# One block of 128 rows per partition instead of two blocks of 65 and 63 rows, and the logits in one transfer

## The chip, the cores and the metric

The kernel runs on one NeuronCore of one Trainium2 chip. The metric is the time of one execution on the device, in microseconds (us); lower is better. Three runs of the kernel before took 239.15 to 239.20 us, median 239.16 us. The profile comes from one more execution, which took 239.38 us, of which the span that the profile covers is 237.6 us.

## What is computed

The reference is the gate of a mixture of experts. For each of 16 x 1024 tokens it takes the softmax over 8 logits, keeps the two largest probabilities, scales them to a sum of one, and writes the token's 512 values twice, once times each of the two weights, the smaller first:

```
probs = np.exp(router_logits - logits_max)
probs = probs / np.sum(probs, axis=-1, keepdims=True)
topk_indices = np.argsort(probs, axis=-1)[..., -k:]
topk_probs = np.take_along_axis(probs, topk_indices, axis=-1)
topk_probs = topk_probs / np.sum(topk_probs, axis=-1, keepdims=True)
x_expanded = x[:, :, np.newaxis, :].repeat(k, axis=2)
return (x_expanded * topk_probs[..., np.newaxis]).astype(np.float32)
```

With k = 2, x is 16 x 1024 x 512 float32 (33.55 MB, 2048 B a token), the logits are 16 x 1024 x 8 float32 (0.52 MB, 32 B a token), and the output is 16 x 1024 x 2 x 512 float32 (67.11 MB, 4096 B a token).

## The kernel before

The 16384 tokens are "rows" here. They are spread over the 128 partitions of the on-chip memory, 128 rows to each (M = 128), in two groups: GROUPS = [65, 63] (line 16). Group 0 is the first 128 x 65 rows of x, and partition p has rows 65 p to 65 p + 64 of it; group 1 is the remaining 128 x 63 rows, and partition p has rows 63 p to 63 p + 62 of those. Lines 87 to 94 build these views of x, output and logits: x_v, o_v and rl_v, one entry a group. So what one partition reads in one transfer is one contiguous run of memory, and the runs of neighbouring partitions lie a fixed distance apart, which this document calls the pitch. The pitch is the group's rows times the bytes of a row:

| | group 0 | group 1 |
|---|---|---|
| x | 65 x 2048 B = 130 KiB | 63 x 2048 B = 126 KiB |
| output | 65 x 4096 B = 260 KiB | 63 x 4096 B = 252 KiB |
| logits | 65 x 32 B = 2080 B | 63 x 32 B = 2016 B |

Tiles on the chip: xs holds up to 65 rows of x per partition, osp has space for 18 rows of output (OSP), and WA holds the two weights of every row. The logits are loaded into the last row of osp, and the scratch space of the selection is the two rows ahead of it.

What runs, in the order in which it is issued:

- Loads: all by SyncE (SP), line 112, in pieces of LOADS = [[6, 28, 31], [32, 31]] rows per partition. After the piece of 6 rows, SP issues the two transfers of logits (lines 105 and 106), then the pieces of 28 and 31 rows.
- Weights: top2_weights works on the logits of both groups at once on VectorE (DVE), with max and min over halves (lines 53 to 66), and takes the two sigmoids of the difference on ScalarE (ACT), lines 67 and 68. Its first instruction, line 53, waits for both transfers of logits.
- Products and stores: STORES (lines 23 to 37) lists by hand, for each group, pieces of 2, 16, 16, 16 and 15 rows (group 1: 16, 16, 16, 15), the place where a piece's products go (osp, or rows of xs that have been used up), how many of its rows ACT multiplies (line 135) while DVE multiplies the rest (line 127), and the queue that issues the store (line 138): ACT's for the first piece, SP's for all others.
- The loads of group 1 overwrite xs. The one of 32 rows waits for the store of the second 16-row piece of group 0, which has its products in xs, and the one of 31 rows waits for the store of the last 15 rows.

A transfer is spread over the core's 16 DMA engines by partition, and each partition's run is one packet of up to 64 KiB (32 rows of x, or 16 rows of output); one more small packet per engine reports the end of the transfer. That makes 128 + 16 = 144 packets a transfer, and 16 x 144 = 2304 in all, the number on the page.

Of the kernel before, what the change touches and what calls it, by code (L numbers as in the profile page):

```python
# [1 line left out]

# [4 lines left out]

F32 = mybir.dt.float32
ALU = mybir.AluOpType
ACTF = mybir.ActivationFunctionType  # L10
P = 128
E = 8
D = 512


GROUPS = [65, 63]
M = sum(GROUPS)


LOADS = [[6, 28, 31], [32, 31]]  # L20


STORES = [
    [
        (2, ("osp", 0), 0, "ACT"),
        (16, ("osp", 2), 0, "SP"),
        (16, ("x", 2), 0, "SP"),
        (16, ("osp", 0), 4, "SP"),
        (15, ("x", 35), 0, "SP"),
    ],  # L30
    [
        (16, ("osp", 0), 1, "SP"),
        (16, ("x", 0), 0, "SP"),
        (16, ("osp", 0), 4, "SP"),
        (15, ("x", 33), 0, "SP"),
    ],
]
OSP = 18


def top2_weights(nc, scratch, logits, WA):

    used = [0]

    def cut(n):
        a = scratch[:, used[0] : used[0] + M * n].rearrange("p (m n) -> p m n", n=n)
        used[0] += M * n
        return a

    a, b = logits[:, :, 0:4], logits[:, :, 4:8]  # L50
    hi = cut(4)
    lo = b
    nc.vector.tensor_tensor(hi, a, b, op=ALU.max)  # L53
    nc.vector.tensor_tensor(lo, a, b, op=ALU.min)  # L54
    n = 4
    while n > 1:
        n //= 2
        a, b = hi[:, :, 0:n], hi[:, :, n : 2 * n]
        nhi, nlo, tmp = cut(n), cut(n), cut(n)
        nc.vector.tensor_tensor(tmp, lo[:, :, 0:n], lo[:, :, n : 2 * n], op=ALU.max)  # L60
        nc.vector.tensor_tensor(nlo, a, b, op=ALU.min)  # L61
        nc.vector.tensor_tensor(nlo, nlo, tmp, op=ALU.max)  # L62
        nc.vector.tensor_tensor(nhi, a, b, op=ALU.max)  # L63
        hi, lo = nhi, nlo
    dlt = cut(1)
    nc.vector.tensor_tensor(dlt, hi, lo, op=ALU.subtract)  # L66
    nc.scalar.activation(WA[:, :, 0], dlt[:, :, 0], ACTF.Sigmoid, scale=-1.0)  # L67
    nc.scalar.activation(WA[:, :, 1], dlt[:, :, 0], ACTF.Sigmoid, scale=1.0)  # L68


@with_exitstack
def kernel(
    ctx: ExitStack,
    tc: tile.TileContext,
    x: bass.AP,
    router_logits: bass.AP,
    k: bass.AP,
    out: bass.AP,
):
    nc = tc.nc  # L80
    N = x.shape[0] * x.shape[1]
    assert int(k) == 2 and router_logits.shape[-1] == E and x.shape[2] == D
    assert N == P * M
    xf = x.rearrange("b s d -> (b s) d")
    of = out.rearrange("b s k d -> (b s) k d")
    rf = router_logits.rearrange("b s e -> (b s) e")
    x_v, o_v, rl_v = [], [], []
    t0 = 0
    for n in GROUPS:
        t1 = t0 + P * n  # L90
        x_v.append(xf[t0:t1].rearrange("(p m) d -> p m d", p=P))
        o_v.append(of[t0:t1].rearrange("(p m) k d -> p m k d", p=P))
        rl_v.append(rf[t0:t1].rearrange("(p m) e -> p m e", p=P))
        t0 = t1

    pool = ctx.enter_context(tc.tile_pool(name="pool", bufs=1))
    xs = pool.tile([P, max(GROUPS), D], F32)
    osp = pool.tile([P, OSP, 2, D], F32)
    WA = pool.tile([P, M, 2], F32)

    logits = osp[:, OSP - 1].rearrange("p k d -> p (k d)").rearrange("p (m e) -> p m e", e=E)
    scratch = osp[:, OSP - 3 : OSP - 1].rearrange("p r k d -> p (r k d)")

    def load_logits():
        nc.sync.dma_start(logits[:, : GROUPS[0]], rl_v[0])  # L105
        nc.sync.dma_start(logits[:, GROUPS[0] :], rl_v[1])  # L106

    m0 = 0
    for g, G in enumerate(GROUPS):
        r = 0  # L110
        for n in LOADS[g]:
            nc.sync.dma_start(xs[:, r : r + n, :], x_v[g][:, r : r + n, :])  # L112
            if g == 0 and r < 6 <= r + n:
                load_logits()
                top2_weights(nc, scratch, logits, WA)
            r += n
        assert r == G
        r = 0
        for n, (home, a), by_act, queue in STORES[g]:
            if home == "x":  # L120
                og = xs[:, a : a + 2 * n, :].rearrange("p (r k) d -> p r k d", k=2)
            else:
                og = osp[:, a : a + n]
            v = n - by_act
            w = WA[:, m0 + r : m0 + r + n, :]
            if v:
                nc.vector.tensor_tensor(  # L127
                    og[:, :v],
                    xs[:, r : r + v, :].unsqueeze(2).to_broadcast([P, v, 2, D]),
                    w[:, :v].unsqueeze(3).to_broadcast([P, v, 2, D]),  # L130
                    op=ALU.mult,
                )
            for i in range(v, n):
                for c in range(2):
                    nc.scalar.activation(  # L135
                        og[:, i, c], xs[:, r + i, :], ACTF.Copy, scale=w[:, i, c : c + 1]
                    )
            {"SP": nc.sync, "ACT": nc.scalar}[queue].dma_start(o_v[g][:, r : r + n], og)  # L138
            r += n
        assert r == G  # L140
        m0 += G


# [1 line left out]
_INS = ['x', 'router_logits', 'k']  # L145
_OUTS = [((16, 1024, 2, 512), 'float32')]

_NUMBERS = {'k': 2}


# [26 lines left out]
```

## Time and profile before

| | |
|---|---|
| median of 3 runs | 239.16 us (239.15 to 239.20) |
| the profiled execution | 239.38 us, span 237.6 us |
| bytes read and written | 34.08 MB and 67.11 MB |
| transfers | 5 loads of x, 2 of logits, 9 stores |
| DVE busy | 132.2 us (56% of the span) |
| ACT busy | 13.2 us (6%) |

How to read what is shown below. The page of the profile begins with the busy time of each engine; its second part cuts the span into 40 equal slices, with the mean busy share of the 16 DMA engines in tenths and the GB/s that they moved. The chain of waits goes back from the last instruction and names at each step what released it. The timeline lists instructions by start and duration, SPq being the queue of SyncE, whose time is that of issuing and not of moving data. The view by stretches gives, for chosen stretches of the span, the busy time of the engines, the granted TensorE clock (not used by this kernel), the share that the DMA engines were busy, and GB/s. A packet takes up to some us and seems to be credited whole to the stretch where it falls, so that short stretches swing above and below what was really moved (a share above 1.00 can be met); long ones are better.

### The profile page before, as it was taken

Reading aid. Unit: us, or ns where it says so; the run is one execution under the profiler, and the core shown is the slowest. Engines: PE = TensorE matmul, PEld = TensorE weight load, DVE = VectorE, ACT = ScalarE, POOL = GpSimd, SP = SyncE. Lnnn points to the kernel's source line nnn. Section 1 sums busy time; section 2 is a strip of 40 time slices with the busy share of each in tenths; the row PEclk is TensorE's granted clock in tenths of the full one; section 3 lists DMA queues with packets and bytes.
Section 4 is the critical chain, followed back from the end, with each engine's and each line's share of the span. In section 5 each row is a group of like instructions: output and inputs, shape, how many; then the busy total and the mean of one; then the engine's idle time right before and its main releaser. Section 6 shows DMA issues by size and latency. Waiting matters only on the chain.

```text
span 237.6 us, 124 instructions
## 1 busy us (share of the span) xinstructions
DVE 132.2 (56%) x20; ACT 13.2 (6%) x21; POOL 0.2 (0%) x4
## 2 busy tenths in 40 slices
DVE  0640599999289999000000009999956999920000
ACT  2000000000080000000000001000006100000000
POOL 0000000000000000000000000000000000000000
DMA  7979989898989989899998989898989989897995
GB/s 265 541 338 488 408 386 535 348 530 353 496 386 441 441 353 530 353 508 414 414 519 353 508 370 502 353 519 353 496 386 419 463 353 530 353 530 342 496 445 217
DMA packets 2304, 101.19 MB, mean 426 GB/s; under 512 B 256, under 2 KB 384, under 8 KB 512
## 3 DMA queue, kind: packets, MB, share of 16 engines
q1 hardware_dynamic: 2160, 100.14, 97.7%
q10 hardware_dynamic: 144, 1.05, 1.0%
HBM read 34.08 MB, written 67.11 MB: 426 GB/s over the span
## 4 chain that ended last, share of the span: by engine, by line
DMA 48%; DVE 39%; SPq 1%; issue 0%; DVEq 0%
DMA xs<-in_x_dram 30%; DVE osp L127 25%; DMA out_dram<-osp 19%; DVE xs L127 14%; SPq L105 0%; SPq L106 0%; SPq L112 0%; SPq L138 0%; DVEq L127 0%
## 5 line engine op out<-in xcount | busy, mean ns | idle before, releaser
L127 DVE TENSOR_TENSOR osp<-xs,WA 128x12288 f32<-128x12288 f32 (+3 forms) x5 | 61.6, 12318 | 68.7 <-DMA xs<-in_x_dram 58.4
L127 DVE TENSOR_TENSOR xs<-xs,WA 128x16384 f32<-128x16384 f32 (+1 forms) x4 | 66.8, 16692 | 0.3
L135 ACT ACTIVATE osp<-xs,WA 128x512 f32<-128x512 f32 x18 | 11.4, 709 | 161.3 <-DMA out_dram<-osp 90.0
L53 DVE TENSOR_TENSOR osp<-osp 128x512 f32<-128x512 f32 x1 | 0.7, 692 | 8.2 <-DMA osp<-in_router_logits_dram 8.2
L67 ACT ACT_TABLE_LOAD x1 | 1.3, 1283 | 0.7 <-PEq L158 0.7
L67 ACT ACTIVATE WA<-osp 128x128 f32<-128x128 f32 x1 | 0.3, 316 | 10.1 <-DVE osp L66 10.1
L54 DVE TENSOR_TENSOR osp<-osp 128x512 f32<-128x512 f32 x1 | 0.7, 693 | 0.0
L60 DVE TENSOR_TENSOR osp<-osp 128x256 f32<-128x256 f32 (+1 forms) x2 | 0.7, 352 | 0.0
L62 DVE TENSOR_TENSOR osp<-osp 128x256 f32<-128x256 f32 (+1 forms) x2 | 0.7, 352 | 0.0
L63 DVE TENSOR_TENSOR osp<-osp 128x256 f32<-128x256 f32 (+1 forms) x2 | 0.7, 352 | 0.0
L61 DVE TENSOR_TENSOR osp<-osp 128x256 f32<-128x256 f32 (+1 forms) x2 | 0.7, 351 | 0.0
L66 DVE TENSOR_TENSOR osp<-osp 128x128 f32<-128x128 f32 x1 | 0.3, 292 | 0.0
L68 ACT ACTIVATE WA<-osp 128x128 f32<-128x128 f32 x1 | 0.3, 298 | 0.0
L158 POOL MEMSET const-bfloat16-1.0<- 128x1 bf16 x1 | 0.1, 102 | 0.0
L158 POOL MEMSET const-uint8-127<- 128x1 uint8 x1 | 0.1, 102 | 0.0
L158 POOL MEMSET const-float32-0.0<- 128x1 f32 x1 | 0.1, 99 | 0.2 <-issue 0.2
L158 POOL MEMSET const-float32-1.0<- 128x1 f32 x1 | 0.1, 99 | 0.0
## 6 DMA issues: line engine op xcount, KB each, us to landing
xs<-in_x_dram SPq DMA_DIRECT2D x2, 7936.0 KB, 40.8
out_dram<-xs SPq DMA_DIRECT2D x2, 7680.0 KB, 27.5
xs<-in_x_dram SPq DMA_DIRECT2D x1, 7168.0 KB, 24.2
xs<-in_x_dram SPq DMA_DIRECT2D x1, 1536.0 KB, 6.0
out_dram<-osp ACTq DMA_DIRECT2D x1, 1024.0 KB, 24.5
osp<-in_router_logits_dram SPq DMA_DIRECT2D x1, 260.0 KB, 6.2
osp<-in_router_logits_dram SPq DMA_DIRECT2D x1, 252.0 KB, 6.4
out_dram<-osp SPq DMA_DIRECT2D x4, 23.9
```

The costliest lines, as they stand in the source:

```text
L53: nc.vector.tensor_tensor(hi, a, b, op=ALU.max)
L54: nc.vector.tensor_tensor(lo, a, b, op=ALU.min)
L60: nc.vector.tensor_tensor(tmp, lo[:, :, 0:n], lo[:, :, n : 2 * n], op=ALU.max)
L61: nc.vector.tensor_tensor(nlo, a, b, op=ALU.min)
L62: nc.vector.tensor_tensor(nlo, nlo, tmp, op=ALU.max)
L63: nc.vector.tensor_tensor(nhi, a, b, op=ALU.max)
L66: nc.vector.tensor_tensor(dlt, hi, lo, op=ALU.subtract)
L67: nc.scalar.activation(WA[:, :, 0], dlt[:, :, 0], ACTF.Sigmoid, scale=-1.0)
L68: nc.scalar.activation(WA[:, :, 1], dlt[:, :, 0], ACTF.Sigmoid, scale=1.0)
L127: nc.vector.tensor_tensor(og[:, :v], xs[:, r : r + v, :].unsqueeze(2).to_broadcast([P, v, 2, D]), w[:, :v].unsqueeze(3).to_broadcast([P, v ...
L135: nc.scalar.activation(og[:, i, c], xs[:, r + i, :], ACTF.Copy, scale=w[:, i, c : c + 1])
L158: nc = _bacc.Bacc("TRN2", target_bir_lowering=False, num_devices=1)
```

## The change

x and output are seen as one block of 128 rows for each partition (xp and op): partition p has rows 128 p to 128 p + 127, of which the first 65 are its share of group 0 and the other 63 of group 1. The entries of x_v and o_v are slices of those views. The pitch becomes 128 x 2048 B = 256 KiB for x and 128 x 4096 B = 512 KiB for the output, for both groups. The logits come in one transfer, 128 x 32 B = 4096 B per partition, and rl_v is gone. The pieces of loads and stores, the tiles, the queues and the arithmetic are as before. A blank line more near the top and three lines less further down shift the numbers of some lines: lines 53 to 68 of before are 54 to 69 after, the one transfer of logits is line 106, and from line 108 on the numbers are the same.

```
-    x_v, o_v, rl_v = [], [], []
+    xp = xf.rearrange("(p m) d -> p m d", p=P)
+    op = of.rearrange("(p m) k d -> p m k d", p=P)
+    x_v, o_v = [], []
     t0 = 0
     for n in GROUPS:
-        t1 = t0 + P * n
-        x_v.append(xf[t0:t1].rearrange("(p m) d -> p m d", p=P))
-        o_v.append(of[t0:t1].rearrange("(p m) k d -> p m k d", p=P))
-        rl_v.append(rf[t0:t1].rearrange("(p m) e -> p m e", p=P))
-        t0 = t1
+        x_v.append(xp[:, t0 : t0 + n])
+        o_v.append(op[:, t0 : t0 + n])
+        t0 += n
...
     def load_logits():
-        nc.sync.dma_start(logits[:, : GROUPS[0]], rl_v[0])
-        nc.sync.dma_start(logits[:, GROUPS[0] :], rl_v[1])
+        nc.sync.dma_start(logits, rf.rearrange("(p m) e -> p m e", p=P))
```

## The prediction

> **What bounds the kernel now.** I read the page's second part first, then the view by stretches, the chain of waits, and the timeline of the start.
>
> ```profile
> span 237.6 us, 124 instructions
> DVE 132.2 (56%) x20; ACT 13.2 (6%) x21; POOL 0.2 (0%) x4
> DMA  7979989898989989899998989898989989897995
> DMA packets 2304, 101.19 MB, mean 426 GB/s; under 512 B 256, under 2 KB 384, under 8 KB 512
> q1 hardware_dynamic: 2160, 100.14, 97.7%
> q10 hardware_dynamic: 144, 1.05, 1.0%
> HBM read 34.08 MB, written 67.11 MB: 426 GB/s over the span
> ...
> 0.00:2.00 2.00, 0.00 (x0) 1.27 (x1) 0.20 (x4) 1.00 0.35 68
> 4.00:6.00 2.00, 0.00 (x0) 0.00 (x0) 0.00 (x0) 1.00 0.97 415
> 2.00:43.00 41.00, 22.76 (x13) 0.52 (x3) 0.00 (x0) 1.00 1.00 426
> 44.00:95.00 51.00, 45.78 (x3) 5.01 (x8) 0.00 (x0) 1.00 1.00 432
> 100.00:140.00 40.00, 0.00 (x0) 0.00 (x0) 0.00 (x0) 1.00 1.00 433
> 235.00:236.00 1.00, 0.00 (x0) 0.00 (x0) 0.00 (x0) 1.00 0.00 0
> ```
>
> No slice of the DMA line is empty, and the two queues together took 98.7% of what sixteen engines could give. In the long stretches, mostly loads in the first, stores in the second, both mixed in the third, the share is 1.00; the rate is 426 GB/s with the start in it and then 432 and 433. At 432 GB/s the 101.19 MB take 101.19 / 432 = 234.2 us. The span has 237.6; the other 3.4 us are the start (the row 0 to 2 us has a share of 0.35, the first load being issued only at 0.73) and the end (nothing is carried after 235). So the time is bytes over rate plus 3.4 us, and no gap is left to close between the first packet and the last. DVE works 132.2 us and is 44% idle; the chain shows what that idleness waits for:
>
> ```profile
> 2.10 24.16 DMA xs<-in_x_dram
> ...
> 26.35 17.24 DVE osp L127
> ...
> 43.61 22.22 DMA out_dram<-osp
> ...
> 95.58 46.42 DMA xs<-in_x_dram
> ...
> 158.32 21.80 DMA out_dram<-osp
> ...
> 193.26 16.16 DVE xs L127
> ```
>
> Each long step of DVE follows a landing of a load or of a store. A slower transfer therefore moves everything behind it by the same amount, and a faster one would do so too; the chain's pieces are only the places where DVE notices.
>
> **The logits.** One transfer in place of two.
>
> ```profile
> 0.73 0.38 SPq L112 DMA_DIRECT2D xs<-in_x_dram  x1
> 1.16 0.43 SPq L105 DMA_DIRECT2D osp<-in_router_logits_dram  x1
> 1.64 0.42 SPq L106 DMA_DIRECT2D osp<-in_router_logits_dram  x1
> 2.10 1.11 SPq L112 DMA_DIRECT2D xs<-in_x_dram  x2
> 8.16 0.69 DVE L53 TENSOR_TENSOR osp<-osp 128x512 f32<-128x512 f32 x1 [8.16 <-DMA osp<-in_router_logits_dram]
> 12.63 2.29 DVE L127 TENSOR_TENSOR osp<-xs,WA 128x2048 f32<-128x2048 f32 x1 [0.58 <-ACT WA L68]
> 14.95 0.37 ACTq L138 DMA_DIRECT2D out_dram<-osp  x1
> ...
> xs<-in_x_dram SPq DMA_DIRECT2D x1, 1536.0 KB, 6.0
> osp<-in_router_logits_dram SPq DMA_DIRECT2D x1, 252.0 KB, 6.4
> ```
>
> SP issues one instruction less: 2.10 - 1.64 = 0.46 us, by which the loads of 28 and 31 rows are issued earlier. That is worth nothing by itself: the load of 6 rows lands at 0.73 + 6.0 = 6.7 us and the engines are busy with it until about then, more than 4 us after the next loads are in the queue. Without that cover it would be the whole 0.46 us. On the engines the bytes stay the same (512 KB). The second transfer of logits lands at 1.64 + 6.4 = 8.0, which leaves 8.0 - 6.7 = 1.3 us for 0.524 MB, against 0.524 / 432 = 1.2 us at the long stretches' rate. What packets of 2 KB and the second report of completion cost is thus at most 0.1 us, and one transfer with 128 + 16 packets less (2304 becomes 2160) cannot save more. I take the 0.1 us, since the engines are the bound and pass it on to the end; its own bounds are 0 and 0.1. On DVE's side line 53 now waits for one transfer; it may start 0.1 us earlier, and so may the first store at 14.95, which shares the engines with loads that are queued in any case.
>
> **The order and the waits.** In the order of instructions every engine has what it had, but for that one issue: DVE 20 operations with the same shapes, ACT its 18 products, nine stores and five loads with the same pieces. The waits on SP's queue stand where they stood: the load of 32 rows waits for the second 16-row store of group 0, the load of 31 rows for the 15-row store, and behind these two wait the stores of group 1. The semaphores that transfers report to go round, and with one transfer less all later ones move by one place; each wait still names the same transfer. No wait is added, so 0 with no bounds to keep.
>
> **The pitch.** This is the part that can matter. What the 16 engines do at the same time is to walk through the runs of 16 different partitions. Before, the starts of neighbouring runs lie 130 or 126 KiB (x) and 260 or 252 KiB (output) apart; only runs 64 or 128 partitions apart have the low 18 bits of their addresses in common. After, all lie 256 KiB and 512 KiB apart: every run starts with the same low 18 (x) or 19 (output) bits. If the memory picks its parallel parts by those bits, engines that are in step ask the same part together. The trace of before has no transfer with such a pitch, so I bound the price. Below: 0, as in the rows of 432 and 433 GB/s, where the engines are the limit; a gain is excluded, since a share of 1.00 leaves none. Above: the only time when all engines are surely in step is the first load, which they begin together. Its first microseconds hold the wait for the first data as well:
>
> ```profile
> 2.00:4.00 2.00, 0.00 (x0) 0.01 (x1) 0.00 (x0) 1.00 0.80 307
> ...
> 5.00:6.00 1.00, 0.00 (x0) 0.00 (x0) 0.00 (x0) 1.00 0.91 387
> ```
>
> At 307 GB/s throughout, the bytes would take 101.19 / 307 = 329.6 us, 95 us more; that is the outermost end and I give it little weight, as most of that row's loss is the wait for first data. In the next two microseconds (row 4 to 6) the packets flow and the engines are still nearly in step, at 415 GB/s. At that rate the output alone takes 67.11 / 415 - 67.11 / 432 = 6.4 us more and x and logits 34.08 / 415 - 34.08 / 432 = 3.2 us more, together 9.6 us. Between 0 and 9.6, nearest to these rows and far from 95, I take the middle, 4.8 us, which is three quarters of what the output, whose pitch is the longer one, would lose alone. It falls on the end in full, because the engines have no pause in which to hide it: later stores first lengthen DVE's two waits for osp (5.11 and 4.64 us) and SP's wait of 26.2 us ahead of the loads of group 1.
>
> ```profile
> 65.95 12.96 DVE L127 TENSOR_TENSOR osp<-xs,WA 128x12288 f32<-128x12288 f32 x1 [5.11 <-DMA out_dram<-osp]
> 180.22 12.96 DVE L127 TENSOR_TENSOR osp<-xs,WA 128x12288 f32<-128x12288 f32 x1 [4.64 <-DMA out_dram<-osp]
> SPq L112 <- DMA out_dram<-xs: 26.2, 1, 26.2
> ```
>
> The Trainium skill has a rule that speaks against this change: DMA: Bandwidth & Descriptors, section Latency and other measured facts, entry on HBM row pitch at large powers of two. Copies between memory tensors gave 207 GB/s in each direction at a pitch of 512 KiB per partition, 164 at 2 MiB, 103 at 4 MiB, and 214 again at 4 MiB padded by 4 KiB; the page calls its mechanism an inference. That before runs at 432 GB/s with pitches 4 KiB off 256 KiB agrees with the padded case; no run here yet shows the other. Taken for the output alone, the rule would give an estimate of 155.3 x (214 / 207 - 1) = 5.3 us more, so a sum of 244.6 us, while the unchanged row of 432 GB/s gives 239.3.
>
> **The sum.** Against the profiled execution of 239.38 us: 239.38 - 0.1 + 0 + 4.8 = 244.1. The median of the runs is 0.22 us under the profiled execution, so the forecast is 243.9 us.
>
> **The rivals.**
>
> The addresses don't matter: the DMA engines set the pace whatever the pitch. For it speaks that the share stays at 1.00 in loads, stores and their mixture, through four different pitches. Against it, that none of the four is a power of two. It gives 239.16 - 0.1 = 239.1 us, no change that can be told. It decides wherever the memory serves each engine's packets faster than the engine asks.
>
> The engines stay in step for good and loads suffer as well. The steps that then grow are the waits for loads in the chain (24.16 and 46.42 us) before the stores. At the worst later microsecond of the first load, 387 GB/s in the row 5 to 6, the bytes take 101.19 / 387 = 261.5 us, 27.3 more: 266.4 us. For it: the rates of 432 and 433 GB/s are so steady that engines, once in step, seem to have little to pull them out of it. Against it: a single microsecond with whole packets credited to it is a poor witness.
>
> The front is shorter: faster. The logits' one issue brings the loads to the engines 0.46 us earlier and the engines start the load of 28 rows that much sooner, with the 0.1 us of packets on top: 239.16 - 0.56 = 238.6 us. It needs the engines to have run dry between 4 and 8 us; the row 4 to 6 with a share of 0.97 speaks against it, and so does the load's landing at 6.7 us.
>
> That the change doesn't do what it says can be left out: the pitches are fixed by the views.
>
> **How the numbers follow.** A moderate loss by the pitch: 0.56, between 239.7 and 250 us. Engines in step for good: 0.12, 250 and above. No effect: 0.26, at 239.1. The shorter front: 0.06, at 238.6. I give the pitch more than half because it changes for every byte at a moment when the transfers have no slack, and the one stretch in which engines are in step is slow. Measured runs differ by 0.05 us, and 0.2% (0.5 us) is about what can be told from no change; faster 0.06, within 0.26, slower 0.68. The range goes from 238.9, just under the case of no effect, to 253, which takes in the 9.6 us at 415 GB/s (248.7) and the beginning of the strong case; the rest of that, about 0.1, and the shorter front are left out. The likeliest case's own range is 239.7 to 250.
>
> **What would show it.** If the forecast holds, the DMA line of the page stays full, the mean falls from 426 to about 417 GB/s with the same MB, and the long stretches show a share of 1.00 at less than 432 GB/s; DVE's busy time stays at 132.2 us. The chain's waits for a store (22.22 and 21.80 us) grow by some 0.6 us for 16 rows, an eighth of 4.8. If the pitch does nothing, the stretches still show 432. The step on the logits is right if line 106 is issued once, the next load at about 1.6 us, and the first weights begin at about 8.1 us. The forecast is wrong if loads slow down and stores don't, or if gaps (shares well under 1.00 in a long stretch) appear.

## The result and the profile after

The changed kernel takes 240.35 us (median of 6 runs, 240.16 to 240.75); the kernel before took 239.18 us in the runs beside it (6 runs, 239.15 to 239.28). The ratio is 1.005, 95% interval 1.0037 to 1.0063. It is slower, as forecast, and inside the range, but by 1.17 us where 4.8 were forecast. The profiled execution took 240.16 us, the lowest of its six; so the profile shows 0.78 us of the loss.

From the page of the kernel after, the span, the DMA line and the totals; then its view by stretches (stretch, its length, busy time of DVE, ACT and POOL, clock, DMA share, GB/s):

```profile
span 238.4 us, 122 instructions
DMA  7979989898989898989798999998999989897994
DMA packets 2160, 101.19 MB, mean 424 GB/s; under 512 B 240, under 2 KB 240, under 8 KB 368
...
44.00:95.00 51.00, 45.79 (x3) 5.01 (x8) 0.00 (x0) 1.00 1.00 432
100.00:140.00 40.00, 0.00 (x0) 0.00 (x0) 0.00 (x0) 1.00 1.02 433
116.00:128.00 12.00, 0.00 (x0) 0.00 (x0) 0.00 (x0) 1.00 1.06 426
```

The bytes are the same, the packets are 144 fewer, and the stretch from 44 to 95 us, where little but stores at the new pitch of 512 KiB is moved, runs at a share of 1.00 and 432 GB/s, to the digit what it was. So a stream of stores does not suffer from the pitch at all. The stretch from 100 to 140 moves the same 433 GB/s, but the engines were busy for 1.02 in place of 1.00. The time between 116 and 128 us holds the difference. The same stretch of the kernel before:

```profile
116.00:128.00 12.00, 0.00 (x0) 0.00 (x0) 0.00 (x0) 1.00 0.99 426
```

Equal bytes (426 GB/s), but the packets took 0.07 x 12 = 0.84 us of every engine's time more. What happens there is read from the chain of waits of the kernel after (start, length, what):

```profile
1.63 24.49 DMA xs<-in_x_dram
...
43.47 22.21 DMA out_dram<-osp
...
95.44 47.27 DMA xs<-in_x_dram
...
158.95 21.88 DMA out_dram<-osp
...
193.97 16.16 DVE xs L127
```

and from its timeline, with the two loads of group 1 in one row whose length runs from the issue of the first to the issue of the second:

```profile
1.16 0.42 SPq L106 DMA_DIRECT2D osp<-in_router_logits_dram  x1
1.63 0.95 SPq L112 DMA_DIRECT2D xs<-in_x_dram  x2
8.12 0.69 DVE L54 TENSOR_TENSOR osp<-osp 128x512 f32<-128x512 f32 x1 [8.12 <-DMA osp<-in_router_logits_dram]
95.44 28.63 SPq L112 DMA_DIRECT2D xs<-in_x_dram  x2
```

In the kernel before the last of these rows was:

```profile
95.58 27.65 SPq L112 DMA_DIRECT2D xs<-in_x_dram  x2
```

At 95.4 us the kernel after is 0.14 us ahead. By the end of the chain's next piece, at 95.44 + 47.27 = 142.7 against 142.0, it is 0.7 us behind, and it stays so: the last step of DVE begins at 193.97 against 193.26. The waits for stores are 22.21 and 21.88 us, against 22.22 and 21.80. The whole loss lies in one piece: the landing of the last 15 rows of group 0, for which the second load waits, comes 28.63 - 27.65 = 1.0 us later. That is the only place in the kernel where the engines change from a long run of stores to loads.

The trace also keeps the size, start and length of every packet, and these narrow it down. In the kernel after, each of the 16 engines carries the 15-row store as eight packets. The last one takes 2.63 to 2.97 us, where the seven ahead of it take 2.27; the first two packets of the load behind it take 2.42 to 2.95 us, where later ones take 2.42. Together that is 0.9 us an engine. In the kernel before, the same packets take at most 2.38 and 2.53 us. The packets of the long stream of stores take 2.42 us in both kernels, although the 16 engines begin theirs within 0.5 us of each other all through it.

### The profile page after: what moved, and what is told of

Read it like the earlier page. It is cut to its first block, busy times and chain, and to the rows that moved or that the text cites. A ratio compares the mean times of both kernels' runs of the same rounds, so it can differ in the third digit from the quotient of the medians.

```text
span 238.4 us, 122 instructions
## 1 busy us (share of the span) xinstructions
DVE 132.2 (55%) x20; ACT 13.2 (6%) x21; POOL 0.2 (0%) x4
## 4 chain that ended last, share of the span: by engine, by line
DMA 49%; DVE 38%; SPq 0%; issue 0%; DVEq 0%
DMA xs<-in_x_dram 30%; DVE osp L127 25%; DMA out_dram<-osp 18%; DVE xs L127 14%; SPq L106 0%; SPq L112 0%; SPq L138 0%; DVEq L127 0%
```

## The experiments

The times of each group were taken on one chip with runs of the kernel before among them. The row that is shown for each is that of the two loads of group 1, as above, because its length tells the loss without the noise of the rest.

**Which part of the change.** Four kernels, each with one part of the change alone or undone.

The pitch of x alone (x_v from one block, the rest as before):

```
-        x_v.append(xf[t0:t1].rearrange("(p m) d -> p m d", p=P))
+        m0 = t0 // P
+        x_v.append(xf.rearrange("(p m) d -> p m d", p=P)[:, m0 : m0 + n])
```

> x is read from one block of 128 rows per partition (pitch 256 KiB), output and logits as before, so that the rows of x that are multiplied are other ones than those that the weights belong to. Theory A (the loss needs both pitches, because it arises where the stores of the last 15 rows of group 0 meet the loads of group 1 and both have the same low address bits): about 239.2 us, and SP's wait ahead of the load of 31 rows stays at 26.2 us. Theory B (the pitch of the output alone): 239.2 us. Theory C (the pitch of x alone): about 240.4 us, the wait at 27 us. Theory D (the one transfer of logits, which moves the engines' phases): 239.2 us.

The pitch of the output alone:

```
-        o_v.append(of[t0:t1].rearrange("(p m) k d -> p m k d", p=P))
+        m0 = t0 // P
+        o_v.append(of.rearrange("(p m) k d -> p m k d", p=P)[:, m0 : m0 + n])
```

> The output is written as one block of 128 rows per partition (pitch 512 KiB), x and logits as before, so that rows land in other places than the reference's. Theory A (both pitches needed): about 239.2 us, SP's wait ahead of the load of 31 rows at 26.2 us. Theory B (output alone): about 240.4 us, the wait at 27 us. Theory C (x alone): 239.2 us. Theory D (logits): 239.2 us.

The one transfer of logits alone:

```
-        nc.sync.dma_start(logits[:, : GROUPS[0]], rl_v[0])
-        nc.sync.dma_start(logits[:, GROUPS[0] :], rl_v[1])
+        nc.sync.dma_start(logits, rf.rearrange("(p m) e -> p m e", p=P))
```

> The logits come in one transfer of 4096 B per partition, x and output as before, so that most rows get the weights of others. Theories A, B and C: 0.1 us faster than before, about 239.1 us, with the first weights at 8.1 us. Theory D (the one transfer moves the engines' phases and that costs at the change from stores to loads): about 240.4 us.

The changed kernel with two transfers of logits:

```
-        nc.sync.dma_start(logits, rf.rearrange("(p m) e -> p m e", p=P))
+        rl = rf.rearrange("(p m) e -> p m e", p=P)
+        nc.sync.dma_start(logits[:, : GROUPS[0]], rl[:, : GROUPS[0]])
+        nc.sync.dma_start(logits[:, GROUPS[0] :], rl[:, GROUPS[0] :])
```

> The changed kernel with the logits in two transfers again, from the one block (2080 and 2016 B per partition at a pitch of 4096 B). Theories A, B and C: as slow as the changed kernel or 0.1 us slower, 240.4 to 240.5 us, the load of 31 rows waiting about 27 us. Theory D (logits): about 239.2 us.

| | us (median, range) | ratio to before, 239.23 us |
|---|---|---|
| x alone | 239.68 (239.57 to 239.88) | 1.0018 (1.0009 to 1.0026) |
| output alone | 240.78 (240.30 to 241.00) | 1.0059 (1.0047 to 1.0072) |
| logits alone | 239.31 (239.22 to 239.49) | 1.0003 (0.9994 to 1.0011) |
| x and output, two transfers of logits | 240.71 (240.39 to 240.82) | 1.0056 (1.0043 to 1.0070) |

The row of the two loads of group 1, from the timelines in this order:

```profile
95.85 27.56 SPq L113 DMA_DIRECT2D xs<-in_x_dram  x2
```

```profile
95.36 28.71 SPq L113 DMA_DIRECT2D xs<-in_x_dram  x2
```

```profile
95.36 27.60 SPq L111 DMA_DIRECT2D xs<-in_x_dram  x2
```

```profile
96.05 28.52 SPq L114 DMA_DIRECT2D xs<-in_x_dram  x2
```

The two kernels with the output at 512 KiB have 28.5 to 28.7 us there, the two without it 27.6, as before. Theory A falls: x need not have its new pitch. Theories C and D fall as well; B, the output alone, stands, and x and logits add nothing to it that can be told. One thing none of the theories said: x alone costs 0.45 us. Its profile has the first load land 0.3 us later than before, which is not in the changed kernel. From the views of DMA issues (KB, us to landing) of x alone and of the kernel after:

```profile
xs<-in_x_dram SPq DMA_DIRECT2D x1, 1536.0 KB, 6.3
```

```profile
xs<-in_x_dram SPq DMA_DIRECT2D x1, 1536.0 KB, 6.1
```

**Low bits or distance.** The pitch of 512 KiB is a power of two, and it is also twice the old one. Two kernels with everything else as before, in both of which the last store is cut into 13 and 2 rows, have 128 and 126 rows from one partition's output to the next; in both, rows land elsewhere than the reference's. The two excerpts leave out the lines that cut the last store.

```
+    op = of.rearrange("(p m) k d -> p m k d", p=P)
+    o_v = [op[:, :65], op[:, 65:126]]
+    o_tail = op[:, 126:]
...
```

> x and logits as before, output at a pitch of 512 KiB (128 rows), the last store cut into 13 and 2 rows so that it can be compared with its sister of 504 KiB. Both theories: the loss of the output's pitch is there, about 1.5 us over the time that its sister would have without it, so about 241 us; the chain's piece of waiting for the loads of group 1 at about 48 us.

```
+    op = of[: P * 126].rearrange("(p m) k d -> p m k d", p=P)
+    o_v = [op[:, :65], op[:, 65:]]
+    o_tail = of[P * 126 :].rearrange("(p m) k d -> p m k d", p=P)
...
```

> The same with the output at a pitch of 504 KiB (126 rows; the two rows of each partition that are left over go to the end of the output, so rows land elsewhere than the reference's). Theory low bits (what costs is that all runs start with the same low 19 address bits): 1.2 to 1.5 us faster than the kernel with 512 KiB, the piece of waiting for the loads of group 1 at about 46.5 us. Theory distance (what costs is that neighbouring partitions lie twice as far apart): the same time as with 512 KiB, the piece at about 48 us.

512 KiB: 240.51 us (240.31 to 240.60), ratio 1.0049 (1.0037 to 1.0062) to before, 239.30 us. 504 KiB: 239.22 us (239.12 to 239.61), ratio 1.0000 (0.9991 to 1.0009). The same row from the timelines of 512 and of 504 KiB:

```profile
95.30 28.71 SPq L116 DMA_DIRECT2D xs<-in_x_dram  x2
```

```profile
95.54 27.53 SPq L116 DMA_DIRECT2D xs<-in_x_dram  x2
```

8 KiB less of nearly the same distance takes the whole loss away. It is the low bits.

A third kernel asked whether half the pitch is enough, with two groups of 64 rows:

```
-GROUPS = [65, 63]
+GROUPS = [64, 64]
-LOADS = [[6, 28, 31], [32, 31]]
+LOADS = [[6, 28, 30], [32, 32]]
...
-        (15, ("x", 35), 0, "SP"),
+        (14, ("x", 35), 0, "SP"),
...
-        (15, ("x", 33), 0, "SP"),
+        (16, ("x", 32), 0, "SP"),
```

> Before with two groups of 64 rows each: pitches of 128 KiB for x and 256 KiB for the output, both powers of two but half of the changed kernel's; loads of 6, 28, 30 and 32, 32 rows, stores of 2, 16, 16, 16, 14 and four of 16 rows. All right results. If 18 equal low bits in the output's addresses are enough for the loss: about 240.5 us, the piece of waiting for the loads of group 1 over 47 us. If it takes the 19 bits of 512 KiB: about 239.2 us, the piece at 46.5 us. Between them: a smaller pitch costs less.

239.61 us (239.38 to 240.35), ratio 1.0018 (1.0009 to 1.0027) to 239.21 us, between the two: some 0.4 us. Since the sizes of two stores and two loads differ as well, and x has a pitch of 128 KiB, this is no clean number; it suggests that 256 KiB costs less than 512, and doesn't show it.

**Once per change from stores to loads?** If the loss belongs to that change, a kernel with one change more should lose about twice. The load of 32 rows is cut into 16 and 16, and the first is issued ahead of the last store of group 0; this for the old pitches and for the output at 512 KiB.

```
-LOADS = [[6, 28, 31], [32, 31]]
+LOADS = [[6, 28, 31], [16, 16, 31]]
...
+            if g == 0 and n == 15:
+                n1 = LOADS[1][0]
+                nc.sync.dma_start(xs[:, :n1, :], x_v[1][:, :n1, :])
             {"SP": nc.sync, "ACT": nc.scalar}[queue].dma_start(o_v[g][:, r : r + n], og)
```

> Before, with the load of 32 rows of group 1 cut into 16 and 16, and the first 16 issued ahead of the store of the last 15 rows of group 0, so that the engines change from stores to loads twice in place of once. Both theories: 239.2 us, up to 0.2 us more for one transfer more; it is the reference for its sister with the other output pitch.

> The same with the output at a pitch of 512 KiB. Theory change (each change of the engines from stores to loads costs about 1.5 us at this pitch, and nothing else costs): about 3 us over its sister with the old pitches, 242.2 us. Theory place (something about this one store or this one moment costs, or the loss is spread): about 1.5 us over its sister, 240.7 us.

Old pitches: 240.21 us (239.98 to 240.63), ratio to before (239.30 us) 1.0041 (1.0029 to 1.0054), more than the 0.2 us that I had allowed for one transfer more; why was not followed up. Output at 512 KiB (rows land elsewhere): 243.65 us (243.00 to 244.08), ratio 1.0177 (1.0161 to 1.0192). The difference of the sisters is 3.4 us, against 1.5 us with one change. The view by stretches of the old pitches, and then of 512 KiB, around the two changes from stores to loads and around the change from the last load back to stores:

```profile
96.00:108.00 12.00, 0.00 (x0) 0.00 (x0) 0.00 (x0) 1.00 1.02 437
124.00:140.00 16.00, 7.13 (x1) 0.00 (x0) 0.00 (x0) 1.00 0.96 414
156.00:168.00 12.00, 4.15 (x1) 0.00 (x0) 0.00 (x0) 1.00 1.01 433
```

```profile
96.00:108.00 12.00, 0.00 (x0) 0.00 (x0) 0.00 (x0) 1.00 0.99 393
124.00:140.00 16.00, 8.08 (x1) 0.00 (x0) 0.00 (x0) 1.00 0.99 400
156.00:168.00 12.00, 6.62 (x1) 0.00 (x0) 0.00 (x0) 1.00 0.93 371
```

Share and GB/s are to be read together: 1.02 for 437 is the normal price of a byte (1.00 for 432), 0.99 for 393 is 9% over it, 0.99 for 400 is 7% over, 0.93 for 371 is 8% over. Each change from stores to loads costs again, as theory "change" had it. But the third row is a change from loads to stores, which costs nothing in the kernel after (share 1.04 at 449 GB/s from 156 to 168 us). Here the store has been in the queue for some 29 us when the last load lands; in the kernel after it is 2.5 us. So the direction is not the whole of it. The chain shares out the 3.4 us; first the old pitches, then 512 KiB:

```profile
95.05 38.03 DMA out_dram<-xs
...
133.53 47.53 DMA out_dram<-osp
```

```profile
95.08 40.32 DMA out_dram<-xs
...
135.85 48.65 DMA out_dram<-osp
```

The first piece, in which both changes from stores to loads fall, is 2.3 us longer; the second, in which the change back to stores falls, 1.1 us. So it is about 1 us at each of three places and not 1.5 at each of two. Theory "place" falls, and of theory "change" the part falls by which nothing else costs.

**Overlap or restart.** Two explanations were left: stores and loads that are in flight together get in each other's way, or engines that begin on another tensor need some packets to sort themselves out. In the next pair no load of group 1 is issued before the last store of group 0 has landed, because that store's products are moved down to overlap the first load's rows. They then overlap the rows of the second 16-row store as well, so that DVE waits for that store too (24.30 and 24.27 us in the chains of the two kernels); this delays both alike.

```
-        (15, ("x", 35), 0, "SP"),
+        (15, ("x", 31), 0, "SP"),
```

> Before, with the products of the last 15 rows of group 0 put 4 rows lower in xs (row 31 in place of 35), so that they overlap the first load of group 1 too and that load is issued only once the store has landed: the engines finish the stores, run dry for a moment, and start on the loads. Both theories: about 2 us over before, 241.2 us, for the landing and the issue that now lie bare; it is the reference for its sister.

> The same with the output at a pitch of 512 KiB. Theory overlap (the loss arises only while stores and loads are in flight at the same time): no loss is left at this place, so the same time as its sister within 0.3 us. Theory restart (engines that begin on another tensor lose some packets' time until they have sorted themselves out, with or without stores in flight): about 1 us or more over its sister.

Old pitches: 241.88 us (241.59 to 242.10). Output at 512 KiB (rows land elsewhere): 241.96 us (241.66 to 242.18). The ratios to before (239.21 us) are 1.0111 (1.0097 to 1.0125) and 1.0116 (1.0100 to 1.0131): the loss is gone from the difference. The chain of the old pitches and of 512 KiB:

```profile
101.21 21.11 DMA out_dram<-xs
122.34 22.25 DMA xs<-in_x_dram
```

```profile
101.21 21.11 DMA out_dram<-xs
122.34 22.11 DMA xs<-in_x_dram
```

The 15 rows land after 21.11 us in both, and the load after 22.25 and 22.11. With the load issued only after the store has landed, the pitch costs nothing there: theory "restart" falls, and "overlap" stands. What the pair shows is that the loss needs the load queued behind the store. That data of both are then under way at once is my reading and isn't shown: by the packet records of the kernel after, the first packet of the load begins only at 122.0 us, when the first of the slow packets of the store ends. What the separation itself costs (2.7 us) is more than it saves, so it is no remedy.

## Why the prediction was right in sign and four times too large

**What bounds the kernel: right.** The DMA line stayed full, DVE waited, and 0.8 to 1.0 us of longer packets at 116 to 128 us came through to the end in full: 0.7 us late at 142, and 0.8 us more span.

**The logits: right, and too small to tell.** Line 106 is issued once, the next load at 1.63 us, and DVE's first instruction begins at 8.12 in place of 8.16. Logits alone give 1.0003 (0.9994 to 1.0011), which holds the 0.1 us gain and no gain as well. The shorter front, the faster rival, is refuted by the same kernel.

**The order and the waits: right.** Every wait stands where it stood, and apart from what follows from it only the one whose store lands late ends later than before. Of the three waits that the prediction expected to grow, SP's did, from 26.2 to 27.1 us; DVE's two for osp did not (5.11 and 4.71 us, against 5.11 and 4.64).

**The pitch: the mechanism was right in kind, its size was not.** The low bits are what costs (504 KiB against 512 KiB). The step that failed is the price: "Between 0 and 9.6, nearest to these rows and far from 95, I take the middle, 4.8 us". Behind it stood the picture of engines that are in step and slow for as long as they run, taken from the first load's 415 GB/s. But the engines are in step through the whole stream of stores, within 0.5 us, and lose nothing there. Measured, the term is about 1.2 to 1.6 us (1.17 for the whole change, 1.55 for the output alone, 1.29 between 512 and 504 KiB). The long stream of stores at 512 KiB ran at 432 GB/s, so that the loss, which I spread over all 101 MB, arises only where a load is queued behind a store, and there in about three packets of each engine. The first load's 415 GB/s was no witness for it; it was there before, without any such pitch. The two signs that I had named for a moderate loss, long stretches under 432 GB/s and longer waits for stores, both failed, and the loss appeared in the chain's wait for loads, which I had kept for the strong rival.

The rule of the Trainium skill (DMA: Bandwidth & Descriptors, Latency and other measured facts) pointed the right way: by it a pitch of 512 KiB costs, and a pad of 4 KiB (on 4 MiB) restores the rate. Here 512 KiB cost 1.29 us and 504 KiB nothing, so these runs agree with it in kind. The estimate of 5.3 us that the prediction worked out from it was too large. Its figures are for copies between two memory tensors. Such a copy has reads and writes throughout, while in this kernel they meet mainly at the changes; that this explains the difference is my reading, and no run here copied memory to memory.

**What stays open.** Why x alone costs 0.45 us while x beside the output adds nothing to it; the profile puts 0.3 us at the first load, in one execution. Why the change from loads to stores costs in the kernel with the divided load and not in the kernel after; the store's long wait in the queue is a difference between them, and that it is the cause wasn't tried. Why the store of 2 rows, which ACT's queue moves among the loads of group 0 from 20 to 36 us, loses nothing at 512 KiB (its 8 KiB packets take 0.309 us in both kernels): its small packets and its own queue set it apart, and neither was tried. Which part of the memory the equal low bits share wasn't seen either; the runs show only that it takes stores with equal low bits and loads queued behind them.

## What to carry to other kernels

Ask of a power-of-two pitch not what rate a stream has, but where stores and loads follow each other in the queue: a stream alone showed no loss at 512 KiB, and each change from a long run of stores to loads cost about a microsecond. Where DMA is the bound, a layout in which the blocks of neighbouring partitions lie a few KiB off a power of two (here 63 or 65 rows, or 126, in place of 128) removes it for nothing. When a rate is carried from a row to a forecast, ask first for how many microseconds the condition of that row will hold.

## What was not expected of the hardware

Equal low 19 bits in the starts of 128 store runs do no harm to a stream of stores (432 GB/s, share 1.00). Where a load is queued behind the stores, the last packet of the store and the first two of the load take up to 2.97 us in place of 2.27 and 2.42, which is 0.9 us an engine. Neither the packets before nor those after show it.
